# Two-layer hybrid recurrent trunk: gate weights stacked in one operand and interleaved with the first query tile, x loaded slice first, last tile and final norm by quarters

## The chip, the cores and the metric

The kernel runs on one core of a Trainium2 chip. The metric is device microseconds of one execution: the median of three runs before the change is 2355.97 us (2355.65 to 2356.04). A profile of one further execution stands beside them.

## The reference: what is computed

Two layers over 512 frames of width 1024, all in float32. Each layer normalises x (RMS), projects it with one large matrix, and feeds two branches, an mLSTM with four heads and a retention with four heads; a gated merge, a feed-forward block and a gated embedding are each added to x. At the end stands one more norm. What the change touches:

```python
h = rmsnorm(x, norm1_g[i])
z = h @ w_in[i] + b_in[i]
_, _, mv, mo, mi, mf, rq, rk, rv, rg, gm, gr = split_cols(z)   # mi, mf: 4 columns each
...
h3 = rmsnorm(x, norm3_g[i])
x = x + jax.nn.sigmoid(h3 @ w_pe_gate[i]) * (p[i] @ w_pe[i])   # the last step of a layer
return rmsnorm(x, final_g)
```

`mi` and `mf` are the input and forget gates of the mLSTM: 8 columns in all, of some 12,300.

## The kernel before

**Layout.** Activations lie transposed: eight tiles `x[0..7]` of 128 channels by 512 frames. Every float32 operand is split into a high part (`h`, a rounded copy, made by ScalarE, L286) and a low part (`l`, the rest, made by VectorE, L287), and every product is three matmuls: high by high, low by high, high by low (`mm3`, L423 to L425). An output tile of 128 channels (`t8`, L427) is 8 slices of 3 matmuls, 24 in all, each with 512 moving columns. The matmuls named in the profile by L423 to L425 are these.

**Weights.** They come in a fixed order of units (`unit_list`, L151): SyncE loads a block of 128x1024 (`wr`, 512 KB) into one of four or five raw buffers (`fill_raws`), ScalarE and VectorE split it into `wh` and `wl` two units ahead of its use (`unit`, `LOOK` = 2), in a ring of six buffers. All engines work in order, each on its own queue.

**Start.** TensorE runs 20 matmuls on ones (`WARM`, L863). SyncE loads the first weight block (unit `IF`: the 8 gate columns of the projection, set in a block of 128 columns that is zero otherwise), then x[0] to x[7]; ScalarE's queue loads the per-channel vectors `bc`. For each slice ScalarE makes `l0n1h` (L604) and VectorE `l0n1l` (L605): the operand is x times the gain, and the norm's factor is applied to the results later. TensorE then runs the gate tile (`l0if`, 24 matmuls, L911 to L913) and four query and key tiles of head 0 (`l0m0z`, L1155). Meanwhile ScalarE squares the slices (L618), and GpSimd adds up the squares (L626; the last one is added by VectorE, L624). After the second of those tiles TensorE sums over channels (`finish`, L633), VectorE and GpSimd form the factor, and after the third tile it is spread over the partitions (`spread`, L662). `gate_rows` (L783) then turns the gate tile into rows of decays with some twenty small operations on ScalarE and VectorE, and the evacuation of the query and key tiles follows on the same engines.

**Between the layers.** The last eight tiles of layer 0 (`l0pg`) are evacuated by `pe_evac` (L1417): multiply by the norm's factor, sigmoid, multiply by `pe`, add to x, then the operand of the next layer's norm (`l1n1h`, `l1n1l`). The gate tile and the query tiles of layer 1 follow at once.

**End.** In layer 1 the last four tiles are computed in two halves of 256 frames (`pl`, L1462), so that the final norm of the first half (`n40`) lies beside the matmuls of the second. For the second half (`n41`) stand at the very end: the evacuation of tile 7, its square, the sums over channels (L633, L635), the factor (VectorE, GpSimd, L640), two diagonal blocks (L648), a matmul that spreads them (L650), three multiplications (`final`, L1451) and their stores (L1452).

Of the kernel before, what the change touches and what calls it, by code (L numbers as in the profile page):

```python
# [42 lines left out]
P = 128  # L43
# [11 lines left out]
WARM = 20  # L55
# [180 lines left out]
def build(ctx, tc, ins, out):  # L236
# [34 lines left out]
    nc.scalar.dma_start(bc[:, 0, :], ins["vecs"][0])  # L271
# [85 lines left out]

    def fill_raws(most=RAWS + 1):
        while at["load"] < len(loads) and len(raws) + len(kept) < most:
# [20 lines left out]

    def prep_next():
# [10 lines left out]
        out_ = [pl.tile([P, w], F32R, name=f"w{a}{n}_{nm}", **kw) for a in "hl"]  # L392
# [3 lines left out]
        in_order("prep", *split(r[:, :w], *out_))  # L396
# [186 lines left out]
    class Norm:  # L583
# [23 lines left out]
        def square(self, k, x, pool=False):  # L607
# [7 lines left out]
            if pool:  # L615
                gp.tensor_tensor(sq, x, x, OP.mult)
            else:
                ac.activation(sq, x, AF.Square)  # L618
            if self.sum is None:
                self.sum = sq  # L620
            elif k == KT - 1 and self.n < NT:
                self.tail = sq
            elif k == KT - 1:
                ve.tensor_tensor(self.sum, self.sum, sq, OP.add)  # L624
            else:
                gp.tensor_tensor(self.sum, self.sum, sq, OP.add)  # L626

        def finish(self):
# [11 lines left out]
            gp.tensor_tensor(self.c[:, 0:self.n], ms, nhalf[:, 0:self.n], OP.pow)  # L640

# [141 lines left out]
    def gate_rows(i, o, nrm):  # L783
# [4 lines left out]
        ve.tensor_tensor(f[F_, :T], o[F_, :], nrm.b[F_, :], OP.mult)  # L788
        ac.activation(f[F_, :T], f[F_, :T], AF.Identity, bias=b[F_, :])
        li = tmp(n + "li")  # L790
        ve.tensor_tensor(li[I_, :T], o[I_, :], nrm.b[I_, :], OP.mult)
# [82 lines left out]
    for i in range(L):  # L874
# [279 lines left out]
        for d in range(4):  # L1154
            o = t8(xa, f"l{i}m0z{d}")  # L1155
# [293 lines left out]
    def final(n, c0, c1):  # L1449
        v = whole[:, c0:c1, n.s]  # L1450
        ve.tensor_tensor(v, v, n.b.rearrange("p (a t) -> p a t", a=1).to_broadcast([P, c1 - c0, n.n * P]), OP.mult)  # L1451
        nc.sync.dma_start(out[c0:c1, :, n.s].rearrange("c p t -> p c t"), v)  # L1452
# [6 lines left out]
    for a, n in enumerate(nn):  # L1459
        for c in range(KT - LAST, KT):  # L1460
# [8 lines left out]
            elif a == 1 and c == KT - LAST + 1:  # L1469
                nn[0].whole()  # L1470
            pe_evac(o, c, n.s, [n])
            ac.activation(x[c][:, n.s], x[c][:, n.s], AF.Copy, scale=n.col(c))
            if a == 1 and KT - LAST < c < KT - 1:
                final(nn[0], 4 * (c - KT + LAST - 1), 4 * (c - KT + LAST))
    nn[1].finish()
    nn[1].whole()
    for c0, c1 in ((0, 4), (4, 6), (6, 8)):
        final(nn[1], c0, c1)
# [8 lines left out]
def _pack_units(a):  # L1487
# [7 lines left out]
    for i in range(L):  # L1495
        for u in unit_list(i):
# [3 lines left out]
            elif u[0] in ("PAIR", "WIDE"):  # L1500
# [4 lines left out]
            elif u[0] == "PE":  # L1505
                c = 512 * u[1]
                blocks.append(a["w_pe"][i, :, c:c + T].reshape(2, P, 4, P).transpose(1, 2, 0, 3).reshape(P, UN))
            else:
                z = np.zeros((D, P), np.float32)
                z[:, 0:H] = a["w_in"][i, :, CI:CI + H]  # L1510
                z[:, 32:32 + H] = a["w_in"][i, :, CF:CF + H]
                put(z)
# [92 lines left out]
```

## Time and profile before

| what | us |
|---|---|
| median of three runs | 2355.97 |
| profiled execution, its own time | 2357.84 |
| span of that execution, first to last instruction | 2356.1 |
| TensorE busy in the span | 2328.2 |
| VectorE, ScalarE, GpSimd busy | 1716.9, 1217.9, 252.3 |
| first `l0if` matmul starts | 7.53 |
| `l0n1ss` (sum over channels) starts | 25.50 |
| first `l1if` matmul starts | 1181.57 |
| last matmul on weights starts | 2342.80 |
| last stores issued, DMA queue of SyncE ends | 2352.4 |

Rows of the timeline give the start in us from the span's start, the length in us, the engine, the line, the operation, output and inputs, and in brackets the idle time just before with what ended it. PE is TensorE, DVE VectorE, ACT ScalarE, POOL GpSimd, SP SyncE; a "q" behind a name is the engine's queue of DMA issues. Rows of the groups give busy us and mean ns. Windows give busy us and instructions of each engine in a stretch, then the granted TensorE clock, the DMA engines' share and GB/s. TensorE's matmuls overlap, so their pace is read from start to start.

### The profile page before, as it was taken

Reading aid. Unit: us, or ns where it says so; the run is one execution under the profiler, and the core shown is the slowest. Engines: PE = TensorE matmul, PEld = TensorE weight load, DVE = VectorE, ACT = ScalarE, POOL = GpSimd, SP = SyncE. Lnnn points to the kernel's source line nnn. Section 1 sums busy time; section 2 is a strip of 40 time slices with the busy share of each in tenths; the row PEclk is TensorE's granted clock in tenths of the full one; section 3 lists DMA queues with packets and bytes.
Section 4 is the critical chain, followed back from the end, with each engine's and each line's share of the span. In section 5 each row is a group of like instructions: output and inputs, shape, how many; then the busy total and the mean of one; then the engine's idle time right before and its main releaser. Section 6 shows DMA issues by size and latency. Waiting matters only on the chain. (4 is left out here: it accounts for less than half of the span.)

```text
span 2356.1 us, 35296 instructions
## 1 busy us (share of the span) xinstructions
PE 2328.2 (99%) x13692; PEld 2062.1 (88%) x13692; DVE 1716.9 (73%) x2643; ACT 1217.9 (52%) x1760; POOL 252.3 (11%) x372
## 2 busy tenths in 40 slices
PE   9999999999999999999999999999999999999998
PEld 7888899898898898898888888998989988998997
DVE  6877767886665586677768787778958656776785
ACT  5655544553454445445557564455536445445454
POOL 4111100100102200000321110000000020000012
PEclk9999999999999999999999999999999999999999
DMA  5666676666578766777776645334343443333431
GB/s 202 183 177 169 218 223 182 196 200 189 166 232 265 204 193 184 208 216 182 214 210 175 183 121 183 131 123 162 108 160 105 166 152 98 126 108 99 131 121 54
DMA packets 145319, 395.87 MB, mean 168 GB/s; under 512 B 14960, under 2 KB 17392, under 8 KB 145152
## 3 DMA queue, kind: packets, MB, share of 16 engines
q1 hardware_dynamic: 98928, 248.78, 32.1%
q0 software_dynamic: 31104, 117.45, 20.6%
q10 hardware_dynamic: 15120, 27.40, 3.3%
q8 instruction: 107, 1.75, 0.3%
q14 instruction: 60, 0.49, 0.1%
HBM read 374.69 MB, written 123.73 MB: 212 GB/s over the span
## 5 line engine op out<-in xcount | busy, mean ns | idle before, releaser
L286 ACT ACTIVATE wh<-wr 128x1024 fp32r<-128x1024 f32 x222 | 234.0, 1055 | 298.3 <-issue 64.9
L287 DVE TENSOR_TENSOR wl<-wr,wh 128x1024 fp32r<-128x1024 f32 x222 | 273.6, 1233 | 94.1 <-ACT wh L286 93.8
L286 ACT ACTIVATE wh_B<-wr 128x1024 fp32r<-128x1024 f32 x100 | 105.9, 1059 | 158.1 <-PE l0f L424 8.5
L287 DVE TENSOR_TENSOR wl_B<-wr,wh_B 128x1024 fp32r<-128x1024 f32 x100 | 122.1, 1221 | 31.0 <-ACT wh_B L286 30.8
L286 ACT ACTIVATE wh_D<-wr 128x512 fp32r<-128x512 f32 x76 | 48.0, 632 | 125.9 <-DVE wr L405 67.0
L286 ACT ACTIVATE wh_C<-wr 128x1024 fp32r<-128x1024 f32 x76 | 80.2, 1056 | 61.5 <-issue 8.4
L287 DVE TENSOR_TENSOR wl_C<-wr,wh_C 128x1024 fp32r<-128x1024 f32 x76 | 94.3, 1241 | 19.0 <-ACT wh_C L286 18.8
L286 ACT ACTIVATE wh_A<-wr 128x1024 fp32r<-128x1024 f32 x76 | 79.9, 1052 | 53.9 <-PE l1f L424 9.0
L287 DVE TENSOR_TENSOR wl_A<-wr,wh_A 128x1024 fp32r<-128x1024 f32 x76 | 92.8, 1221 | 17.2 <-ACT wh_A L286 16.7
L423 PE MATMUL l1f<-l1n2h,wh 128*128 128x512 f32 x256 | 99.8, 390 | 0.0
L423 PE MATMUL l0f<-l0n2h,wh 128*128 128x512 f32 x256 | 99.8, 390 | 0.0
L425 PE MATMUL l0f<-l0n2h,wl 128*128 128x512 f32 x256 | 99.7, 389 | 0.0
L425 PE MATMUL l1f<-l1n2h,wl 128*128 128x512 f32 x256 | 99.7, 389 | 0.0
L424 PE MATMUL l0f<-l0n2l,wh 128*128 128x512 f32 x256 | 99.6, 389 | 0.0
L424 PE MATMUL l1f<-l1n2l,wh 128*128 128x512 f32 x256 | 99.6, 389 | 0.0
L287 DVE TENSOR_TENSOR wl_D<-wr,wh_D 128x512 fp32r<-128x512 f32 x76 | 52.4, 690 | 33.7 <-ACT wh_D L286 32.1
L402 DVE TENSOR_TENSOR wr<-wr,wr 128x512 f32<-128x512 f32 x76 | 52.2, 687 | 16.0 <-DMA wr<-wpairs 14.4
L425 PEld LDWEIGHTS l0f<-l0n2h,wl 128*128 128x128 f32 x256 | 48.0, 188 | 10.2
L425 PEld LDWEIGHTS l1f<-l1n2h,wl 128*128 128x128 f32 x256 | 48.0, 188 | 10.2
L423 PEld LDWEIGHTS l0f<-l0n2h,wh 128*128 128x128 f32 x256 | 48.1, 188 | 9.8
L424 PEld LDWEIGHTS l1f<-l1n2l,wh 128*128 128x128 f32 x256 | 48.1, 188 | 9.8
L423 PEld LDWEIGHTS l1f<-l1n2h,wh 128*128 128x128 f32 x256 | 48.0, 188 | 9.7
(5613 smaller groups left out, 8370.1 us busy)
## 6 DMA issues: line engine op xcount, KB each, us to landing
wr<-wstream SPq DMA_DIRECT2D x222, 512.0 KB, 4.4
wr<-wpairs SPq DMA_DIRECT2D x228, 256.0 KB, 2.9
wr<-wwide SPq DMA_DIRECT2D x24, 512.0 KB, 3.6
s0t<-wwide POOLq DMA_DIRECT2D x5, 1024.0 KB, 7.9
s4t<-wwide POOLq DMA_DIRECT2D x5, 1024.0 KB, 8.9
s12t<-wwide POOLq DMA_DIRECT2D x5, 1024.0 KB, 8.6
s16t<-wwide POOLq DMA_DIRECT2D x5, 1024.0 KB, 8.7
s1t<-wpairs POOLq DMA_DIRECT2D x4, 1024.0 KB, 6.7
```

Source lines behind the costliest of these rows:

```text
L286: a = ac.activation(hi_ap, src, AF.Copy)
L287: return a, ve.tensor_sub(lo_ap, src, hi_ap.bitcast(F32))
L402: ve.tensor_tensor(raws[n, "B"][:, Q:], kept.pop((n, "A"))[:, Q:], r[:, :Q], OP.add)
L423: te.matmul(o, sh, mh, start=first, stop=False)
L424: te.matmul(o, sh, ml, start=False, stop=False)
L425: cur["mm"] = te.matmul(o, sl, mh, start=False, stop=last)
```

## The change

In both layers the gate weights are now a block of 128x64 (`wif`, 32 KB). One operand tile `z` is zeroed by GpSimd and holds, per slice, the high part in the columns from 0 and 32 and the low part in the columns from 64 and 96: so two matmuls per slice (one with the high activations, one with the low) give high and low products in different partitions of one PSUM tile. `gate_rows` adds the two parts with a ScalarE copy and a VectorE addition for each gate. The gate tile and the first query tile are now computed together, slice by slice. At the start x[0] is loaded before the first query weights, which come and are split in two halves; the vectors come in two pieces; the warm-up has 11 matmuls; the sums of squares of layer 0's first norm are added by VectorE. At the end tile 7's second half is evacuated in two quarters of 128 frames, and the final norm of the second half (`quarters`) is made for each quarter by itself, with stores of 8x128 and twice 4x128 columns in the place of 4x256 and twice 2x256.

The diff, with the packing on the host and plain renamings left out:

```diff
-WARM = 20
+WARM = 11
...
-    nc.scalar.dma_start(bc[:, 0, :], ins["vecs"][0])
+    nc.scalar.dma_start(bc[:, 0, 0:8], ins["vecs"][0][:, 0:8])
...
+    def halves(n):
+        return [slice(0, Q), slice(Q, UN)] if n == 1 else [slice(0, UN)]
...
+            elif units[n][0] == "IF":
+                eng = nc.sync if n else nc.scalar
+                eng.dma_start(r[:, 0:64], ins["wif"][n * L // NU])
             else:
-                in_order("load", nc.sync.dma_start(r, ins["wstream"][at["whole"]]))
+                w = ins["wstream"][at["whole"]]
+                for c in halves(n):
+                    in_order("load", nc.sync.dma_start(r[:, c], w[:, c]))
...
-        in_order("prep", *split(r[:, :w], *out_))
+        if gates:
+            z = out_[0]
+            gp.memset(z.bitcast(F32), 0.0)
+            z = z.rearrange("p (k g c) -> p k g c", g=4, c=32)
+            split(r[:, 0:64].rearrange("p (k g c) -> p k g c", g=2, c=H), z[:, :, 0:2, 0:H], z[:, :, 2:4, 0:H])
+        elif x == 0:
+            for c in halves(n):
+                in_order("prep", *split(r[:, c], *[a[:, c] for a in out_]))
...
-                gp.tensor_tensor(self.sum, self.sum, sq, OP.add)
+                (add or gp).tensor_tensor(self.sum, self.sum, sq, OP.add)
...
+        def quarters(self):
+            n = self.name
+            o = [ps(f"{n}ss{j}") for j in range(self.n)]
+            r = []
+            for part in (self.sum, self.tail):
+                for j in range(self.n):
+                    te.matmul(o[j][:, 0:2], part[:, j * P:(j + 1) * P], ones[:, 0:2], start=part is self.sum,
+                              stop=part is self.tail)
+            for j in range(self.n):
+                ms = cols.tile([P, NT], F32, name=f"{n}ms{j}", tag="ms")[:, 0:1]
+                ve.tensor_scalar(ms, o[j][:, 0:1], 1.0 / D, EPS, OP.mult, OP.add)
+                c = cols.tile([P, NT], F32, name=f"{n}rc{j}", tag="rc")[:, 0:1]
+                gp.tensor_tensor(c, ms, nhalf[:, 0:1], OP.pow)
+                r.append(c)
+            for j, c in enumerate(r):
+                d = tmp(f"{n}d{j}")[:, 0:P]
+                ve.tensor_scalar(d, ident, c, None, OP.mult)
+                r[j] = ps(f"{n}rp{j}")[:, 0:P]
+                te.matmul(r[j], ones, d, start=True, stop=True)
+            return r
...
-        ve.tensor_tensor(f[F_, :T], o[F_, :], nrm.b[F_, :], OP.mult)
+        li = tmp(n + "li")
+        for d_, s_, e_ in ((f, F_, slice(96, 96 + H)), (li, I_, slice(64, 64 + H))):
+            ac.activation(d_[s_, :T], o[e_, :], AF.Copy)
+            ve.tensor_tensor(d_[s_, :T], o[s_, :], d_[s_, :T], OP.add)
+        ve.tensor_tensor(f[F_, :T], f[F_, :T], nrm.b[F_, :], OP.mult)
...
-    fill_raws(1)
-    for k in range(KT):
+    nc.sync.dma_start(x[0], ins["xT"][0])
+    fill_raws(2)
+    nc.scalar.dma_start(bc[:, 0, 8:NB], ins["vecs"][0][:, 8:NB])
+    for k in range(1, KT):
         nc.sync.dma_start(x[k], ins["xT"][k])
     ready(0)
-    for k in range(KT):
+    n1.operand(0, x[0])
+    ready(1)
+    for k in range(1, KT):
         n1.operand(k, x[k])
...
-        _, wh, wl = unit("IF")
+        _, wi = unit("IF")
+        _, wh, wl = unit("T8")
         og = ps(f"l{i}if")
+        oz = ps(f"l{i}m0z0")
         for k in range(KT):
             s = slice(k * P, (k + 1) * P)
-            mm3(og, wh[:, s], wl[:, s], xa[0][k], xa[1][k], k == 0, k == KT - 1)
+            f, e = k == 0, k == KT - 1
+            te.matmul(og, wi[:, s], xa[0][k], start=f, stop=False)
+            te.matmul(og, wi[:, s], xa[1][k], start=False, stop=e)
+            mm3(oz, wh[:, s], wl[:, s], xa[0][k], xa[1][k], f, e)
         if i == 0:
             for k in range(KT):
-                n1.square(k, x[k])
+                n1.square(k, x[k], ve)
...
-            o = t8(xa, f"l{i}m0z{d}")
+            o = t8(xa, f"l{i}m0z{d}") if d else oz
...
+    def last_evac(o, n):
+        c = KT - 1
+        js = [(slice(j * P, (j + 1) * P), slice((j - 2) * P, (j - 1) * P)) for j in (2, 3)]
+        t = [tmp(f"plt{j}")[:, 0:P] for j in range(2)]
+        n.tail = tmp("pltail")[:, 0:2 * P]
+        for a, (s, q) in zip(t, js):
+            ve.tensor_tensor(a, o[:, q], n3.b[:, s], OP.mult)
+            ac.activation(a, a, AF.Sigmoid)
+        for a, (s, q) in zip(t, js):
+            ve.tensor_tensor(a, a, pe[:, c, s], OP.mult)
+        for a, (s, q) in zip(t, js):
+            ve.tensor_tensor(x[c][:, s], x[c][:, s], a, OP.add)
+            ac.activation(n.tail[:, q], x[c][:, s], AF.Square)
+        for s, q in js:
+            ac.activation(x[c][:, s], x[c][:, s], AF.Copy, scale=n.col(c))
...
+            if a == 1 and c == KT - 1:
+                last_evac(o, n)
+                break
...
-    nn[1].finish()
-    nn[1].whole()
-    for c0, c1 in ((0, 4), (4, 6), (6, 8)):
-        final(nn[1], c0, c1)
+    for j, (b, ends) in enumerate(zip(nn[1].quarters(), ((0, KT), (0, KT // 2, KT)))):
+        for c0, c1 in zip(ends, ends[1:]):
+            final(slice((2 + j) * P, (3 + j) * P), b, c0, c1)
```

How the instructions stand now, at the three places of which the prediction speaks. TensorE at the start, before: the gate tile `l0if` by itself, three matmuls per slice.

```order
L864 MATMUL warm<-ones_r 128x128 x20
L423 MATMUL l0if<-l0n1h_157,wh_0_212 128x512
L424 MATMUL l0if<-l0n1l_158,wh_0_212 128x512
L425 MATMUL l0if<-l0n1h_157,wl_0_213 128x512
L423 MATMUL l0if<-l0n1h_159,wh_0_212 128x512
```

And after (`wh_0_205` is the stacked gate operand, `l0m0z` the first query tile; the numbers behind `l0n1h` and `l0n1l` tell the slices apart):

```order
L905 MATMUL warm<-ones_r 128x128 x11
L961 MATMUL l0if<-l0n1h_157,wh_0_205 128x512
L962 MATMUL l0if<-l0n1l_158,wh_0_205 128x512
L442 MATMUL l0m0z_271<-l0n1h_157,wh_0_213 128x512
L443 MATMUL l0m0z_271<-l0n1l_158,wh_0_213 128x512
L444 MATMUL l0m0z_271<-l0n1h_157,wl_0_214 128x512
L961 MATMUL l0if<-l0n1h_159,wh_0_205 128x512
```

Five matmuls now use a slice where three did, and the first query tile ends with the gate tile. Layer 1 has the same order at its start.

VectorE at the start, before, from the operand of the last slice (`l0n1l_172`) to the first operation on the norm's sum over channels (`l0n1ms`):

```order
L605 SCALAR_TENSOR_TENSOR l0n1l_172<-x_150,bc,l0n1h_171 128x512
L287 TENSOR_TENSOR wl_0_260<-wr_204,wh_0_259 128x1024
L287 TENSOR_TENSOR wl_0_266<-wr_206,wh_0_265 128x1024
L624 TENSOR_TENSOR l0n1sum<-l0n1sum,l0n1sq_314 128x512
L287 TENSOR_TENSOR wl_0_345<-wr_208,wh_0_344 128x1024
L888 CAST l0sel<-l0selraw 36x512
L287 TENSOR_TENSOR wl_0_376<-wr_210,wh_0_375 128x1024
L637 TENSOR_SCALAR l0n1ms<-l0n1ss 128x4
```

And after, the same stretch:

```order
L624 SCALAR_TENSOR_TENSOR l0n1l_172<-x_150,bc,l0n1h_171 128x512
L642 TENSOR_TENSOR l0n1sum<-l0n1sum,l0n1sq_314 128x512
L642 TENSOR_TENSOR l0n1sum<-l0n1sum,l0n1sq_317 128x512
L287 TENSOR_TENSOR wl_0_261<-wr_199,wh_0_260 128x1024
L642 TENSOR_TENSOR l0n1sum<-l0n1sum,l0n1sq_320 128x512
L287 TENSOR_TENSOR wl_0_267<-wr_201,wh_0_266 128x1024
L642 TENSOR_TENSOR l0n1sum<-l0n1sum,l0n1sq_323 128x512
L642 TENSOR_TENSOR l0n1sum<-l0n1sum,l0n1sq_326 128x512
L642 TENSOR_TENSOR l0n1sum<-l0n1sum,l0n1sq_329 128x512
L287 TENSOR_TENSOR wl_0_363<-wr_203,wh_0_362 128x1024
L933 CAST l0sel<-l0selraw 36x512
L640 TENSOR_TENSOR l0n1sum<-l0n1sum,l0n1sq_332 128x512
```

Six additions of squares that GpSimd made now stand among the weight splits, and the last addition stands behind three splits where it stood behind two.

VectorE at the end, before, from the evacuation of tile 7 (`pl`) on:

```order
L1420 TENSOR_TENSOR l1pgt_256_23107<-pl_23082,l1n3rb 128x256
L1422 TENSOR_TENSOR l1pgt_256_23107<-l1pgt_256_23107,l1pe 128x256
L1423 TENSOR_TENSOR l1x<-l1x,l1pgt_256_23107 128x256
L637 TENSOR_SCALAR l1n41ms<-l1n41ss 128x2
L648 TENSOR_SCALAR l1n41d<-ident,l1n41rc 128x128 x2
L1451 TENSOR_TENSOR l1x<-l1x,l1n41rp 128x4x256
L1451 TENSOR_TENSOR l1x<-l1x,l1n41rp 128x2x256 x2
```

And after:

```order
L1511 TENSOR_TENSOR plt_23094<-pl_23069,l1n3rb 128x128
L1511 TENSOR_TENSOR plt_23095<-pl_23069,l1n3rb 128x128
L1514 TENSOR_TENSOR plt_23094<-plt_23094,l1pe 128x128
L1514 TENSOR_TENSOR plt_23095<-plt_23095,l1pe 128x128
L1516 TENSOR_TENSOR l1x<-l1x,plt_23094 128x128
L1516 TENSOR_TENSOR l1x<-l1x,plt_23095 128x128
L669 TENSOR_SCALAR l1n41ms_23115<-l1n41ss_23109 128x1
L669 TENSOR_SCALAR l1n41ms_23119<-l1n41ss_23110 128x1
L675 TENSOR_SCALAR l1n41d_23123<-ident,l1n41rc_23117 128x128
L675 TENSOR_SCALAR l1n41d_23127<-ident,l1n41rc_23121 128x128
L1501 TENSOR_TENSOR l1x<-l1x,l1n41rp_23125 128x8x128
L1501 TENSOR_TENSOR l1x<-l1x,l1n41rp_23129 128x4x128 x2
```

Each step on 256 frames has become two on 128, and the first final multiplication needs only the first quarter's factor. Elsewhere the engines' orders differ only by the operations that the diff names.

More of the change, by code (lines that the diff above doesn't have):

```diff
@@ L391, in prep_next @@
         nm = f"{x[0]}{x[1]}" if wide else x
-        out_ = [pl.tile([P, w], F32R, name=f"w{a}{n}_{nm}", **kw) for a in "hl"]
+        gates = units[n][0] == "IF"
+        out_ = [pl.tile([P, w], F32R, name=f"w{a}{n}_{nm}", **kw) for a in ("h" if gates else "hl")]
         r = formed.pop((n, x), None)
@@ L395, in prep_next @@
             r = raws.pop((n, x))
-        in_order("prep", *split(r[:, :w], *out_))
+        if gates:
[6 more added lines that the diff above has]
+                in_order("prep", *split(r[:, c], *[a[:, c] for a in out_]))
+        else:
+            in_order("prep", *split(r[:, :w], *out_))
         pieces[n, x] = out_
@@ L1504, in _pack_units @@
                 put(a["w_in"][i, 256 * k:256 * k + 256, c:c + T])
-            elif u[0] == "PE":
+            else:
                 c = 512 * u[1]
                 blocks.append(a["w_pe"][i, :, c:c + T].reshape(2, P, 4, P).transpose(1, 2, 0, 3).reshape(P, UN))
[L1508 to L1512, printed above, removed]
     return np.stack(blocks)
```

24 lines of the change are left out of this document (11 added, 13 removed).

## The prediction

> **What bounds the kernel now.** I read the page's sum first, then the windows by stage, then TensorE's waits.
>
> ```profile
> span 2356.1 us, 35296 instructions
> PE 2328.2 (99%) x13692; PEld 2062.1 (88%) x13692; DVE 1716.9 (73%) x2643; ACT 1217.9 (52%) x1760; POOL 252.3 (11%) x372
> 0.00:26.00 26.00, 24.18 (x118) 20.39 (x118) 13.56 (x15) 16.22 (x23) 19.84 (x42) 1.00 0.72 260
> 60.00:1160.00 1100.00, 1088.86 (x6453) 966.83 (x6452) 805.16 (x1233) 563.86 (x815) 128.18 (x176) 1.00 0.69 200
> 1215.00:2336.00 1121.00, 1117.82 (x6670) 994.68 (x6669) 831.52 (x1285) 587.27 (x855) 80.34 (x116) 1.00 0.43 133
> 2343.10:2356.10 13.00, 2.44 (x10) 1.54 (x10) 4.33 (x9) 1.82 (x5) 1.43 (x2) 0.64 0.24 81
> ```
>
> TensorE has work in 99% of the span; in the long middle (60 to 1160, 1215 to 2336) it idles 14 of 2221 us. So an edit counts only where it takes matmuls from TensorE, or where TensorE idles or runs for nothing: the first 26 us (warm-up until 7.5, waits for the first operands) and the last 13 us, where it works 2.44. The change touches these two places and takes 8 matmuls in each layer. A shift of everything behind is worth its full length, since the middle follows TensorE.
>
> **The start, before.** The rows are the first weight block, the slices, the pace of TensorE and the sum over channels.
>
> ```profile
> 1.05 6.73 PE L864 MATMUL warm<-ones_r 128*128 128x128 f32 x40 [1.05 <-POOL ones_r L275]
> 4.89 1.06 ACT L286 ACTIVATE wh<-wr 128x1024 fp32r<-128x1024 f32 x1 [2.37 <-DMA wr<-wstream]
> 7.35 4.05 ACT L604 ACTIVATE l0n1h<-x,bc 128x512 fp32r<-128x512 f32 x6 [0.17 <-DMA x<-xT]
> 7.53 0.47 PE L423 MATMUL l0if<-l0n1h,wh 128*128 128x512 f32 x1
> 13.44 0.50 PE L423 MATMUL l0m0z<-l0n1h,wh 128*128 128x512 f32 x1
> 17.34 0.39 PE L423 MATMUL l0m0z<-l0n1h,wh 128*128 128x512 f32 x1
> 18.02 0.39 PE L423 MATMUL l0m0z<-l0n1h,wh 128*128 128x512 f32 x1
> 22.40 0.69 DVE L624 TENSOR_TENSOR l0n1sum<-l0n1sum,l0n1sq 128x512 f32<-128x512 f32 x1 [5.28 <-POOL l0n1sum L626]
> 25.50 0.95 PE L633 MATMUL l0n1ss<-ones_r,l0n1sum 128*128 128x2 f32 x8
> ```
>
> Matmuls of 512 columns start every (18.02 − 17.34)/3 = 0.227 us. The gate tile starts at 7.53; the first query tile at 13.44, with a hole at its beginning; the sum over channels, `l0n1ss`, at 25.50, right behind the second query tile, and its operand has been ready since 23.1. What counts is therefore when `l0n1ss` starts after the change, as everything behind it keeps its order.
>
> **The start, after.** Two queues can set that point.
>
> ```profile
> 6.00:8.00 2.00, 2.00 (x18) 1.77 (x17) 2.00 (x3) 1.83 (x4) 2.00 (x4) 1.00 1.05 398
> L605 DVE SCALAR_TENSOR_TENSOR l0n1l<-x,bc,l0n1h 128x512 fp32r<-128x512 f32 x8 | 5.4, 738 | 0.0
> L287 DVE TENSOR_TENSOR wl<-wr,wh 128x1024 fp32r<-128x1024 f32 x222 | 273.6, 1233 | 94.1 <-ACT wh L286 93.8
> 24.17 0.43 DVE L888 CAST l0sel<-l0selraw 36x512 fp32r<-36x512 f32 x1
> ```
>
> *TensorE's.* The first weights, 512 KB, were usable at 4.89. x[0] has half of that: usable between 2.5 (half the time) and 4.9 (none of it saved, if the start of the transfers is all that counts); I take 4.2, in the upper half, since no row shows a start-up time apart. ScalarE's high part (0.72, as at 1187.33 below) and VectorE's low part (0.74) follow, then the small gate block (estimate 0.25, as of the 1.06 for 1024 columns at L286 little more than 0.2 can fall on 64): TensorE starts at about 5.9, and the 11 warm-ups end near it (11/20 of 6.7 us gives 4.8; all at their slow first pace 5.8). ScalarE waited for x[2] at 7.35; ahead of x[2] then were 512 KB of weights and two slices, as now, so x[2] is usable at 7.35 again. With 0.72 and 0.74 behind it, TensorE is through with slice 2 at about 9.7. The other five slices arrive faster (262 thousand bytes at 398 GB/s, 0.66 us) than TensorE uses them (5 matmuls, 1.13 us): both tiles end at 9.7 + 5.7 = 15.4, the next query tile 24 × 0.227 = 5.45 later, at **20.85**.
>
> *VectorE's.* x[7] is usable at 7.35 + 5 × 0.66 = 10.65; high and low parts make it 12.1. Behind that stand seven additions of squares (0.69), three weight splits (1.23) and a cast (0.43), one starting some 0.07 before its forerunner's end: 4.8 + 3.7 + 0.45 less 0.7, about 8.3. The sum is ready at **20.5**, with ScalarE's squares no later. The two ends nearly tie; `l0n1ss` starts at about 21.1, a gain of **4.4 us**. Bounds: 5.2 if nothing waits; 0.9 for the half-rate start below.
>
> The hole at the query tile's beginning before was a wait for its split weights; these now come in halves, ahead of the slices but the first. The additions on ScalarE and VectorE in `gate_rows` (two copies, two sums of 512 columns) stand in front of splits that wait anyway:
>
> ```profile
> 32.96 1.23 DVE L287 TENSOR_TENSOR wl<-wr,wh 128x1024 fp32r<-128x1024 f32 x1 [2.09 <-ACT wh L286]
> PE l0m0vp L709 <- DVE wl L287: 1.2, 1, 1.2
> ```
>
> VectorE idles 2.09 us there, and the two sums take, at the 0.69 of L624's row with as many columns, 1.4; ScalarE idles longer still, as that split waits for it and it for TensorE. So I cost them at nothing. Without that cover they would delay VectorE's queue by 1.4 and TensorE's one later wait of this stage (1.2 us, for a split) by as much. The first norm's squares leave GpSimd, which has nothing else that is late. In layer 1 GpSimd zeroes a 128x1024 tile ahead of two additions; it is 11% busy, and nothing waits there.
>
> **Between the layers.**
>
> ```profile
> 1181.57 0.39 PE L423 MATMUL l1if<-l1n1h,wh 128*128 128x512 f32 x1
> 1187.33 0.72 ACT L604 ACTIVATE l1n1h<-l0x,bc 128x512 fp32r<-128x512 f32 x1 [1.49 <-DVE l0x L1423]
> 1188.08 0.75 DVE L605 SCALAR_TENSOR_TENSOR l1n1l<-l0x,bc,l1n1h 128x512 fp32r<-128x512 f32 x1 [0.79 <-ACT l1n1h L604]
> 1188.11 0.50 PE L423 MATMUL l1if<-l1n1h,wh 128*128 128x512 f32 x1
> 1192.89 0.39 PE L423 MATMUL l1m0z<-l1n1h,wh 128*128 128x512 f32 x1
> ```
>
> From 1181.57 TensorE runs the 48 matmuls of gate tile and first query tile; the next tile starts at 1192.89. That is 11.32 us for 48 × 0.227 = 10.9: 0.4 goes where the last slice, ready at 1188.05 and 1188.83, comes late. After the change 40 matmuls need 9.1 us, and the last slice is used only after 35 of them, at 1189.5 on this clock, so it is in time. Gain 11.3 − 9.1 = **2.2 us** (1.8, the 8 matmuls alone, if a wait returns).
>
> **The end.**
>
> ```profile
> 2342.80 0.28 PE L425 MATMUL pl<-l1n3h,wl 128*128 128x256 f32 x1
> 2343.11 0.42 DVE L1420 TENSOR_TENSOR l1pgt<-pl,l1n3rb 128x256 f32<-128x256 f32 x1 [0.44 <-PE pl L425]
> 2345.51 0.38 PE L635 MATMUL l1n41ss<-ones_r,l1n41sq 128*128 128x2 f32 x2 [1.02 <-ACT l1n41sq L618]
> 2346.62 0.71 POOL L640 TENSOR_TENSOR l1n41rc<-l1n41ms,nhalf 128x2 f32<-128x2 f32 x1 [2.57 <-DVE l1n41ms L637]
> 2347.36 0.48 DVE L648 TENSOR_SCALAR l1n41d<-ident,l1n41rc 128x128 f32<-128x128 f32 x2 [0.82 <-POOL l1n41rc L640]
> 2347.89 1.22 PE L650 MATMUL l1n41rp<-l1n41d,ones_r 128*128 128x256 f32 x2 [1.55 <-DVE l1n41d L648]
> 2349.15 2.42 DVE L1451 TENSOR_TENSOR l1x<-l1x,l1n41rp 128x1024 f32<-128x1024 f32 x3 [1.31 <-PE l1n41rp L650]
> 2351.00:2353.00 2.00, 0.00 (x0) 0.00 (x0) 0.57 (x1) 0.00 (x0) 0.00 (x0) 0.50 0.86 284
> 14.60:14.75 0.15, 0.00 (x0) 0.00 (x0) 0.15 (x1) 0.15 (x1) 0.15 (x1) 1.00 0.77 263
> ```
>
> From 2343.11 the chain takes 2.40 to the square's sum, 6.04 to the first final multiplication, 8.46 to the last one's end. With 128 frames a step on VectorE or ScalarE takes about 0.28 (the pair at 2347.36 needs 0.48 for two, against 0.42 for one of 256). The first quarter passes five steps, with the second's step between some of them, in 1.95 in place of 2.40. Its two sums no longer stand behind the other quarter's (0.4 saved); GpSimd's power takes 0.7 as before; one diagonal block is 0.28 in place of 0.48 (0.2); the spreading matmul has half the columns (estimate 0.7, a little over half of 1.22). First final multiplication: 6.04 − 0.45 − 0.4 − 0.2 − 0.5 = 4.5, **1.55 earlier**; the second quarter's chain ends inside its 1.2 us. Multiplications and stores behind it have the same volume. But the stores then run without a hole for three microseconds (284 GB/s in a window that they do not fill), so their rate sets the end, and their rows shrink from 1024 to 512 bytes. Same bytes per time would cost 0, same rows per time 3.1. The only place with rows of 512 bytes is the load of `ident` at 14.6, 263 GB/s with the DMA engines at a share of 0.77, which at a full share is no slower than the stores are: I take 0.25, near zero. Gain **1.3 us** (−1.5 to 2.0).
>
> **Sum.** 4.4 + 2.2 + 1.3 = 7.9 us. The profiled execution's own time, 2357.84 for a span of 2356.1, would become 2349.9; the median of the runs is 1.9 lower than that execution, and I put the gain on it: 2355.97 − 7.9 = **2348.1**.
>
> **The clock.** The granted clock is where another result may come from.
>
> ```profile
> 1.90:5.30 3.40, 3.40 (x18) 1.00 0.91 313
> 5.30:7.50 2.20, 2.20 (x21) 1.00 1.02 383
> 605.00:609.40 4.40, 0.05 (x1) 1.00 0.96 377
> 609.40:616.40 7.00, 6.61 (x30) 0.51 0.12 43
> PE l0r2o1a L472 <- ACT wh_A L286: 4.4, 1, 4.4
> ```
>
> Until 5.3 TensorE passes 18 warm-up records in 3.4 us, then 21 in 2.2: twice the pace, though the column shows 1.00. And behind the one long wait (4.4 us, to 609.4) the clock is half for 7.0 us, although TensorE was busy 6.61 of them. The Trainium skill, "TensorE: Matmul & The Clock Gate", Part 1, says that the clock is half until a free-running window of about 3.4 us was busy throughout, and that the window doesn't begin with the kernel. Both rows agree; the rule speaks against 11 warm-ups, since they last hardly a window and a half.
>
> **Rivals.**
> - *Half rate at the start.* The warm-ups end near 5.5 and TensorE then idles between slices 0, 1 and 2. If a clock that is half needs the 7 us of the row above, from about 6.9 on, TensorE is slow until 13.9: 8.0 us at 0.454 are 17 matmuls, the other 23 take 5.2, both tiles end at 19.1 in place of 15.4, `l0n1ss` comes at 24.6. Start 0.9, all 4.4: 2351.6. For it: half rate held through 94% busy; against it: in this execution the clock rose at 5.3, before the warm-ups end. 0.15.
> - *VectorE becomes the bound of the start.* The adds come behind splits that wait for TensorE's buffers; if the sum is ready at 23 and not at 20.5, the start gives 2.4 and all is 5.9: 2350.1. For it: VectorE has no hole between 12 and 20.5 in my sum; against it: what it waits for is early. 0.13.
> - *The half clock at 609 disappears.* The wait before it stays, but all is moved by 4.4 us, and if the clock then doesn't fall, the 6.61 us of work run at full rate: 3.3 more, 2344.8. For it: the clock fell only at the very end of that wait, at 609.4, so a little less would not do; against it: if executions differ in this at random, the medians don't. 0.12.
> - *Slower.* The clock stays half far beyond the start, because each small hole denies it: it costs 0.5 us for each us, so the gain of 7.9 is gone after some 16 us of half rate beyond 5.9, and slower by 0.2% needs 25, to the third query tile at 31. For it: the 7 us above; against it: TensorE runs without a hole from slice 3 on. 0.04.
>
> **How the numbers follow.** Forecast, gain 6.3 to 9.3: 0.56. The range takes in the forecast, the early clock and the late VectorE down to a gain of 4.8: 2344.8 to 2351.2, over 0.8 in all. A measurement here can tell about 0.2%, 4.7 us, from no change. Faster by more: 0.56 + 0.12 + 0.13 and a little of the first rival, 0.83; within: 0.13; slower: 0.04.
>
> **What would show it.** `l0n1ss` at 21 (24.6 with a granted clock of 0.5 near 8 to 13: first rival; a wait of `l0n1ss` for VectorE: second); 40 matmuls in 9.1 us at the layer boundary without a wait; the last weight matmul 6.6 us earlier in the span; the first final multiplication 4.5 us behind it and the last store's rate near 300 GB/s. Wrong would be: x[0] later than 4.9, a wait in `l0m0vp` beyond 1.2, or another hole of 4 us.

## The result, and the profile after

The changed kernel takes 2348.75 us (median of nine runs, 2347.34 to 2351.17), the kernel before beside it 2355.45 (nine runs, 2353.66 to 2356.97): a ratio of 0.9971, with a 95% interval of 0.9962 to 0.998. That is 6.7 us less, where 7.9 were predicted and 2348.1 stood as the time.

The profiled execution of the changed kernel took 2347.49 with a span of 2345.8, 10.3 less than the span of before. That is more than the medians differ: it lies at the lower end of the change's nine runs, and the one of before, 2357.84, above all nine of its own. So the terms are read from stretches, not from the spans. First the start, TensorE's rows and those of the engines that feed it (start in us, length, engine, line; in brackets the idle time before and what ended it):

```profile
1.05 4.63 PE L905 MATMUL warm<-ones_r 128*128 128x128 f32 x22 [1.05 <-POOL ones_r L275]
3.63 1.28 ACT L623 ACT_TABLE_LOAD   x1 [3.63 <-DMA x<-xT]
4.93 0.72 ACT L623 ACTIVATE l0n1h<-x,bc 128x512 fp32r<-128x512 f32 x1
6.35 0.22 DVE L287 TENSOR_TENSOR wh<-wr,wh 128x64 fp32r<-128x64 f32 x1
6.62 0.50 PE L961 MATMUL l0if<-l0n1h,wh 128*128 128x512 f32 x1 [0.94 <-DVE wh L287]
16.10 0.39 PE L442 MATMUL l0m0z<-l0n1h,wh 128*128 128x512 f32 x1
20.66 0.67 DVE L640 TENSOR_TENSOR l0n1sum<-l0n1sum,l0n1sq 128x512 f32<-128x512 f32 x1
21.54 0.95 PE L649 MATMUL l0n1ss<-ones_r,l0n1sum 128*128 128x2 f32 x8
```

x[0] is there at 3.63, earlier than predicted, but ScalarE then loads its function table for 1.28 us. With the old start (the row is from `e2_tail_only` below) that load lay in the wait for the first weights; now it stands behind the wait for x[0]:

```profile
1.24 1.28 ACT L286 ACT_TABLE_LOAD   x1 [1.24 <-PEq L1637]
```

The first gate matmul comes at 6.62, both tiles end at 16.10, and `l0n1ss` starts at 21.54 in place of 25.50. The sum's last addition ends at 21.33: VectorE and TensorE tie, as predicted.

Between the layers (the first gate matmul, the last slice on ScalarE and on TensorE, the next tile's first matmul, and the sum over channels):

```profile
1175.03 0.39 PE L961 MATMUL l1if<-l1n1h,wh 128*128 128x512 f32 x1
1181.64 0.72 ACT L623 ACTIVATE l1n1h<-l0x,bc 128x512 fp32r<-128x512 f32 x1 [1.49 <-DVE l0x L1473]
1182.96 0.39 PE L961 MATMUL l1if<-l1n1h,wh 128*128 128x512 f32 x1
1184.25 0.40 PE L442 MATMUL l1m0z<-l1n1h,wh 128*128 128x512 f32 x1
1189.73 0.95 PE L649 MATMUL l1n1ss<-ones_r,l1n1sum 128*128 128x2 f32 x8
```

Forty matmuls take 9.22 us where 48 took 11.32: 2.1 saved, and no bracket says that TensorE waited. To `l1n1ss` it is 14.70.

The end (VectorE's evacuation of tile 7 in quarters, the power, the spreading matmuls, the final multiplications, and a window from the last multiplication on):

```profile
2333.83 0.49 DVE L1511 TENSOR_TENSOR plt<-pl,l1n3rb 128x128 f32<-128x128 f32 x2 [0.45 <-PE pl L444]
2336.48 1.09 POOL L671 TENSOR_TENSOR l1n41rc<-l1n41ms,nhalf 128x1 f32<-128x1 f32 x2 [1.71 <-DVE l1n41ms L669]
2337.41 1.39 PE L677 MATMUL l1n41rp<-l1n41d,ones_r 128*128 128x128 f32 x4 [0.99 <-DVE l1n41d L675]
2338.31 2.42 DVE L1501 TENSOR_TENSOR l1x<-l1x,l1n41rp 128x1024 f32<-128x1024 f32 x3 [0.43 <-PE l1n41rp L677]
2340.80:2342.80 2.00, 0.00 (x0) 0.00 (x0) 0.00 (x0) 0.00 (x0) 0.00 (x0) 0.50 1.02 285
```

The first final multiplication starts 4.48 behind the evacuation (6.04 before; 4.5 predicted). But the last one's end lies 5.1 before the span's end (4.5 in the kernel before), and from the evacuation to the span's end it is 11.97 in place of 12.99: of the 1.56 only 1.0 is left. In the window, which they fill, the stores with rows of 512 bytes move 285 GB/s.

In the middle the long wait stands where it stood, and the clock is halved there as before:

```profile
PE l0r2o1a L491 <- ACT wh_A L286: 3.4, 1, 3.4
602.70:609.40 6.70, 5.26 (x23) 4.97 (x24) 5.04 (x11) 3.89 (x9) 0.00 (x0) 0.51 0.45 158
```

### The profile page after: what moved, and what is told of

It reads as the page before. It is cut to its first block, busy times and chain, and to the rows that moved or that the text cites. A ratio compares the mean times of both kernels' runs of the same rounds, so it can differ in the third digit from the quotient of the medians.

```text
span 2345.8 us, 35261 instructions
## 1 busy us (share of the span) xinstructions
PE 2320.2 (99%) x13660; PEld 2056.2 (88%) x13660; DVE 1722.9 (73%) x2658; ACT 1218.9 (52%) x1768; POOL 245.7 (10%) x369
## 5 line engine op out<-in xcount | busy, mean ns | idle before, releaser
L286 ACT ACTIVATE wh<-wr 128x1024 fp32r<-128x1024 f32 (+1 forms) x223 | 232.2, 1044 | 276.5 <-issue 69.6
L287 DVE TENSOR_TENSOR wl<-wr,wh 128x1024 fp32r<-128x1024 f32 (+1 forms) x221 | 271.9, 1232 | 77.7 <-ACT wh L286 77.5
```

What stands on the lines that cost most here:

```text
L286: a = ac.activation(hi_ap, src, AF.Copy)
L287: return a, ve.tensor_sub(lo_ap, src, hi_ap.bitcast(F32))
```

## The experiments

All runs of one group lie on the same chip beside runs of the kernel before, whose median is 2358.03 in the first group (28 runs), 2355.77 in the second (18) and 2356.96 in the third (23). Differences below are against these. The change itself ran beside the others in the second group alone (`e0_again`).

### The end alone, undone and done (first group)

`e1_old_tail`, the change without its end:

```diff
-            if a == 1 and c == KT - 1:
-                last_evac(o, n)
-                break
...
-    for j, (b, ends) in enumerate(zip(nn[1].quarters(), ((0, KT), (0, KT // 2, KT)))):
-        for c0, c1 in zip(ends, ends[1:]):
-            final(slice((2 + j) * P, (3 + j) * P), b, c0, c1)
+    nn[1].finish()
+    nn[1].whole()
+    for c0, c1 in ((0, 4), (4, 6), (6, 8)):
+        final(nn[1].s, nn[1].b, c0, c1)
```

> The changed kernel with the old end (tile 7's second half and its norm on 256 frames at once). Theory, three separate terms on TensorE's path (start 4.0, layer boundary 2.1, end 1.05 by the two traces): only the end is undone, so 1.05 us slower than the change, 5.7 us faster than before; first final multiplication 6.0 us behind the first evacuation of tile 7, span ends 13.0 behind it. Rival, the stores set the end and the quarters bring nothing: as fast as the change, 6.7 us faster than before, with the span's end 12.0 behind the evacuation here too.

`e2_tail_only` is the opposite: the kernel before with these lines as the change has them.

> The kernel before with the new end alone. Theory: 1.05 us faster than before (2354.4), first final multiplication 4.5 us behind the first evacuation of tile 7, span's end 12.0 behind it. Rival, the quarters only move the wait to the stores: no change, span's end 13.0 behind the evacuation.

Measured: 2350.41 for the first (ratio 0.9968, 0.9956 to 0.9979), 2356.44 for the second (0.9994, 0.9985 to 1.0003). One microsecond is below what these intervals tell apart; the traces tell it. First the evacuation and the final multiplications of `e1_old_tail` and its span, then those of `e2_tail_only`:

```profile
2334.49 0.42 DVE L1470 TENSOR_TENSOR l1pgt<-pl,l1n3rb 128x256 f32<-128x256 f32 x1 [0.44 <-PE pl L444]
2340.53 2.42 DVE L1501 TENSOR_TENSOR l1x<-l1x,l1n41rp 128x1024 f32<-128x1024 f32 x3 [1.31 <-PE l1n41rp L688]
span 2347.4 us, 35248 instructions
```

```profile
2341.17 0.49 DVE L1483 TENSOR_TENSOR plt<-pl,l1n3rb 128x128 f32<-128x128 f32 x2 [0.44 <-PE pl L425]
2345.36 2.42 DVE L1473 TENSOR_TENSOR l1x<-l1x,l1n41rp 128x1024 f32<-128x1024 f32 x3
span 2352.9 us, 35309 instructions
```

With the old end the multiplications start 6.04 behind the evacuation and the span ends at 12.9; with the new one 4.19 and 11.7. So the end is worth 1.0 us in the changed kernel (12.9 against 11.97) and about 1.25 in the kernel before (12.99 against 11.7), and the rival, that the stores take it back, holds for a third of it only.

### The eight gate matmuls (first group)

`e3_third_gate` adds a matmul per slice whose result nobody reads:

```diff
             te.matmul(og, wi[:, s], xa[1][k], start=False, stop=e)
+            te.matmul(oy, wi[:, s], xa[0][k], start=f, stop=e)
```

> The changed kernel with one more gate matmul per slice in both layers (into a tile that nobody reads), 16 in all. Theory, matmuls on TensorE's path set the start and the boundary: 16 x 0.227 = 3.6 us slower than the change, 3.1 faster than before; l0n1ss at 23.3 in place of 21.54, and 16.5 us from the first l1if to l1n1ss in place of 14.7. Rival, VectorE's sum of squares (ready at 21.3) sets the start: the eight of layer 0 are covered, l0n1ss stays near 21.5 to 22, the kernel is only 1.8 to 2.2 slower than the change.

Measured: 2351.89 (0.998, 0.9971 to 0.9989).

```profile
23.27 0.95 PE L649 MATMUL l0n1ss<-ones_r,l0n1sum 128*128 128x2 f32 x8
1176.90 0.39 PE L962 MATMUL l1if<-l1n1h,wh 128*128 128x512 f32 x1
1193.22 0.95 PE L649 MATMUL l1n1ss<-ones_r,l1n1sum 128*128 128x2 f32 x8
```

The boundary takes 16.32, 1.62 longer than in the change: nearly the whole 8 × 0.227 = 1.8. `l0n1ss` comes at 23.27, which is 1.73 later than in the first trace of the change, but only 1.0 later than the average of the four traces with this start (22.3, see the next experiment). VectorE's sum was ready at 21.76 and TensorE didn't wait for it, so matmuls lie on the path there too, and the rival (covered by VectorE's sum) is out for this execution; how much of the 1.8 the start pays, one trace can't tell. The whole time shows a smaller loss than the 3.6 expected: the kernel is 6.1 faster than before by the medians and 4.7 by the ratio, where the theory said 3.1.

### The order of the loads (first group)

`e4_old_loads` puts x[0] behind the whole first weight block again:

```diff
-WARM = 11
+WARM = 20
...
-        return [slice(0, Q), slice(Q, UN)] if n == 1 else [slice(0, UN)]
+        return [slice(0, Q), slice(Q, UN)] if n < 0 else [slice(0, UN)]
...
-    nc.sync.dma_start(x[0], ins["xT"][0])
     fill_raws(2)
+    nc.sync.dma_start(x[0], ins["xT"][0])
```

> The changed kernel with the old start of the loads: x[0] behind the whole first weight block, no halves, 20 warm-ups. Theory, the start's gain comes from five matmuls per arriving slice in place of three, the load order only sets the first of them: first gate matmul near 7.6 (6.62 in the change), both tiles end near 16.8, l0n1ss near 22.3, 0.8 to 1 us slower than the change. Rival, the order of the loads carries the start: holes between the slices return, l0n1ss at 24 or later, 2.5 us or more slower than the change.

Measured: 2351.39 (0.9971, 0.9962 to 0.998). The rows are the table load, now behind the wait for the small gate weights, the first gate matmul and the sum:

```profile
5.56 1.28 ACT L286 ACT_TABLE_LOAD   x1 [5.56 <-DMA wr<-wif]
8.30 0.48 PE L961 MATMUL l0if<-l0n1h,wh 128*128 128x512 f32 x1
23.70 0.95 PE L649 MATMUL l0n1ss<-ones_r,l0n1sum 128*128 128x2 f32 x8
```

`l0n1ss` at 23.70 lies between the two theories. Four traces with the change's own start have it at 21.54, 22.37, 22.72 and 22.48, on average 22.3, and two with the old start at 25.5 and 25.6. So by this one trace the old start of the loads costs about 1.4 of the start's 3.3, and the other 1.9 remain with what the edit leaves in place: the stacking with the interleaving, and the additions on VectorE. The edit undoes the order, the halves and the number of warm-ups together, and the table load behind a landing took part in the loss too; the experiment doesn't separate these. The whole time doesn't show the 1.4 at all: the ratio is the change's own, 0.9971, and its interval is wider than that.

### The change again, and fewer warm-ups (second group)

> The changed kernel once more, beside the next three on the same chip: 6.7 us faster than before, l0n1ss between 21.5 and 22.4 (the two starts seen so far differ by 0.8, as the slices of x land at other times).

Measured: 2349.92, 5.9 us less than before (0.9971, 0.996 to 0.9983). This trace shows what differs from execution to execution at the start: the second half of the first weights, and x[7], land later than in the first trace, and TensorE now waits for the sum of squares. The last row, a window at the start, is for comparison with the next run.

```profile
6.88 0.63 ACT L286 ACTIVATE wh<-wr 128x512 fp32r<-128x512 f32 x1 [0.44 <-DMA wr<-wstream]
12.54 0.72 ACT L623 ACTIVATE l0n1h<-x,bc 128x512 fp32r<-128x512 f32 x1 [0.38 <-DMA x<-xT]
22.72 1.05 PE L649 MATMUL l0n1ss<-ones_r,l0n1sum 128*128 128x2 f32 x8 [0.34 <-DVE l0n1sum L640]
6.70:10.10 3.40, 3.08 (x11) 1.95 (x12) 3.01 (x5) 3.12 (x5) 2.97 (x7) 1.00 1.01 380
```

`e5_warm3` has 3 warm-ups:

```diff
-WARM = 11
+WARM = 3
```

> The changed kernel with 3 warm-ups in place of 11. Theory, the clock is granted by windows of about 3.4 us that run free of the kernel, after one that was busy (in five traces it rose between 4.4 and 7.1 us): the warm-ups end near 2.3, so the first busy window lies in the gate tile; TensorE runs at half pace from 6.6 for 3.4 to 6.8 us, l0n1ss comes at 23.2 to 25, the kernel is 1.7 to 3.4 us slower than the change. Rival, some matmuls at the start are enough whatever their number: l0n1ss at 21.5 to 22.4, no difference.

Measured: 2351.76 (0.998, 0.9971 to 0.9989), 1.8 more than the change beside it. The warm-ups, the first gate matmul, the sum, and two windows (the matmuls of TensorE stand in the first pair of brackets):

```profile
1.05 1.65 PE L905 MATMUL warm<-ones_r 128*128 128x128 f32 x6 [1.05 <-POOL ones_r L275]
6.72 0.79 PE L961 MATMUL l0if<-l0n1h,wh 128*128 128x512 f32 x1 [4.02 <-DVE wh L287]
22.89 0.95 PE L649 MATMUL l0n1ss<-ones_r,l0n1sum 128*128 128x2 f32 x8
6.70:10.10 3.40, 3.38 (x8) 2.71 (x9) 3.40 (x6) 3.40 (x7) 3.38 (x6) 1.00 1.06 399
10.20:12.20 2.00, 2.00 (x10) 1.65 (x9) 1.87 (x4) 2.00 (x4) 2.00 (x5) 1.00 0.99 396
```

Eight matmuls in 3.4 us, then ten in 2.0: half pace until about 10. `l0n1ss` is at 22.89 although the slices came early here (VectorE's sum was ready at 21.35). So the first rival of the prediction is real and has this price; with eleven warm-ups or more it was not seen in twelve traces. By the traces' clock records the clock rose between 4.2 and 6.9 us in those twelve, and at 10.0 in this one, 3.3 behind the first gate matmul. The Trainium skill, "TensorE: Matmul & The Clock Gate", Part 1, says that the clock doubles after one busy window of some 3.4 us that runs free of the kernel. This agrees with all thirteen, but the window needn't be busy throughout, as the prediction took it: in `e1_old_tail` the clock rose at 6.74, and TensorE had been busy for 2.78 of the 3.41 us before.

### The table load (second and third group)

`e6_table_early` puts a tiny activation in front, so that the table is loaded while x[0] is on its way:

```diff
     nc.scalar.dma_start(bc[:, 0, 8:NB], ins["vecs"][0][:, 8:NB])
+    early = cols.tile([P, NT], F32, name="early", tag="early")
+    ac.activation(early, nhalf, AF.Copy)
...
-    ready(0)
     n1.operand(0, x[0])
     ready(1)
```

> The changed kernel with one activation of 4 columns in front of ScalarE's first real one, so that the table load (1.28 us, behind the wait for x[0] in the change) lies in that wait. Theory, the table load is on the path to the first matmul: first gate matmul at 5.3 to 5.7 in place of 6.6, l0n1ss up to 1.0 earlier (20.6), the kernel 0.7 to 1.0 us faster than the change. Rival, the landing of the next slices or VectorE's sum sets l0n1ss: first gate matmul as early, but l0n1ss still at 21.3 or later, no gain.

Measured: 2363.39 (1.0031, 1.0019 to 1.0043), 13.5 us more than the change: neither theory had this. The start is as the rival said: first gate matmul at 5.70, then a wait, as the second half of the weights lands at 6.6, and `l0n1ss` at 22.76. The loss lies behind it, in stretches that the edit doesn't touch: 758.7 us from `l1n1ss` to `l1n2ss`, against 754.2 in the change beside it, and TensorE idles only 0.5 more there. In that stretch the 512-column matmuls of the tiles `l1bm`, for example, start every 0.233 us in place of 0.227. The new tile is 16 bytes per partition, but by the layout of the two kernels it moved all tiles laid out behind it by 64: the first weights of `l1bm` lie at byte 42528 in place of 42464, and its activations, which are laid out from the other side, at 122848 in both.

`e10_table_in_place` is made to tell that apart:

```diff
-    early = cols.tile([P, NT], F32, name="early", tag="early")
+    early = cols.tile([P, NT], F32, name="early", tag="ms")
```

> The kernel of e6_table_early with its 16-byte result in a buffer that exists already, in place of a tile of its own: all instructions stand in the same order on all engines, only the tiles laid out behind that tile lie 64 bytes lower, as in the change. Theory, the place of the operands in SBUF cost e6 its 13 us (matmuls of 512 columns every 0.233 us in place of 0.227 wherever weights and activations had moved against each other by 64 bytes): pace 0.227 again, as fast as the change to 1 us, l0n1ss near 22.8 as in e6 (the second half of the first query weights lands at 6.6). Rival, the changed order on ScalarE and VectorE at the start is carried on: still 2363.

Measured: 2350.61 (0.9971, 0.996 to 0.9981). One piece of TensorE's work at the same place of layer 0's feed-forward block, first in `e6_table_early`, then in `e10_table_in_place`, and last a piece of layer 1's block in `e6_table_early`; from the first to the second row of each pair are five steps from matmul to matmul:

```profile
999.61 0.39 PE L444 MATMUL l0f<-l0n2h,wl 128*128 128x512 f32 x1
1000.78 0.39 PE L443 MATMUL l0f<-l0n2l,wh 128*128 128x512 f32 x1
```

```profile
999.67 0.39 PE L444 MATMUL l0f<-l0n2h,wl 128*128 128x512 f32 x1
1000.80 0.39 PE L443 MATMUL l0f<-l0n2l,wh 128*128 128x512 f32 x1
```

```profile
2160.56 0.39 PE L444 MATMUL l1f<-l1n2h,wl 128*128 128x512 f32 x1
2161.70 0.39 PE L443 MATMUL l1f<-l1n2l,wh 128*128 128x512 f32 x1
```

Five steps take 1.17 in the first pair, 1.13 in the second. All instructions of the two kernels stand in the same order on every engine, so the place of the tiles is shown as the cause. The third pair, 1.14, is a control inside one execution: in layer 1 both operands of this block have moved by 64, and the pace is the usual one. With the layout of the change and of `e6_table_early` set beside the starts of their matmuls, some 9,300 gaps behind matmuls of 512 columns whose two operands agree modulo 128 bytes are 0.2274 us on average, and some 3,060 where they differ by 64 are 0.2329. `e6_table_early` has about 2,580 of the second kind and the change 480, so this explains some 12 of the 13 us. The change's own 480 cost it some 2.7 us; the kernel before has them too.

What the table load was worth is shown by three more rows of `e10_table_in_place`:

```profile
5.57 0.50 PE L962 MATMUL l0if<-l0n1h,wh 128*128 128x512 f32 x1
6.60 0.63 ACT L286 ACTIVATE wh<-wr 128x512 fp32r<-128x512 f32 x1 [0.91 <-DMA wr<-wstream]
7.14 0.61 ACT L634 ACTIVATE l0n1sum<-x 128x512 f32<-128x512 f32 x1
```

The first gate matmul comes 1.1 earlier than in the change, but ScalarE then waits for the second half of the weights until 6.60, and `l0n1ss` is at 22.28, the average of the four. (In three of those four ScalarE waits for that half too, until 6.80 to 6.99, with the table load in its old place.) The edit also changed the order: ScalarE now squares x[0] at 7.14, before it makes x[1]'s operand, for which TensorE waits until 8.41. So the load was on the path to the first matmul, and the landing of the weights, with that square behind it, takes its 1.1 back; the two are not separated.

### Who adds the squares (third group)

`e7_gpsimd_sum`:

```diff
-                n1.square(k, x[k], ve)
+                n1.square(k, x[k])
```

> The changed kernel with the sum of squares of layer 0's first norm back on GpSimd (VectorE only the last addition). Theory, the move to VectorE is worth something only as the sum would else come last: six additions of 1.29 to 1.66 us from 12.4 on end at 22.2, the last one at 22.9, l0n1ss at 22.9 to 23.3 waiting for it, 0.4 to 1.4 us later than in the change. Rival, VectorE's queue was itself the bound: without the additions l0n1ss comes at 21.5 or earlier.

Measured: 2351.89 (0.9978, 0.9969 to 0.9987). VectorE's last addition, and the sum over channels:

```profile
23.07 0.69 DVE L640 TENSOR_TENSOR l0n1sum<-l0n1sum,l0n1sq 128x512 f32<-128x512 f32 x1 [5.27 <-POOL l0n1sum L642]
23.82 1.05 PE L649 MATMUL l0n1ss<-ones_r,l0n1sum 128*128 128x2 f32 x8 [1.91 <-DVE l0n1sum L640]
```

TensorE waits 1.91 us for the sum, which is ready at 23.77, later than the 22.9 expected. Compared with the average of 22.3, without the move of the additions to VectorE the faster gate tile would have given back 1.5 of the 3.3 us of the start.

### Rows of 1024 bytes, and a version from all this (second and third group)

`e9_long_rows` keeps the quarters and changes the last multiplications and stores:

```diff
+    q0, q1 = nn[1].quarters()
+    for c0, c1 in ((0, 4), (4, 8)):
+        for j, b in enumerate((q0, q1)):
+            v = whole[:, c0:c1, (2 + j) * P:(3 + j) * P]
+            ve.tensor_tensor(v, v, b.rearrange("p (a t) -> p a t", a=1).to_broadcast([P, c1 - c0, P]), OP.mult)
+        nc.sync.dma_start(out[c0:c1, :, 2 * P:4 * P].rearrange("c p t -> p c t"), whole[:, c0:c1, 2 * P:4 * P])
```

> The changed kernel with the same quarters, but the final multiplications as four of 4x128 columns and two stores of 4x256 (rows of 1024 bytes) in place of three stores with rows of 512. Theory, the short rows cost the end 0.5 us (5.1 us from the last multiplication to the span's end, 4.5 before): 4.5 to 4.6 again, span's end 11.4 behind the first evacuation of tile 7 in place of 12.0, 0.5 us faster than the change. Rival, only the bytes count: the last store is now larger and starts later, so the same or up to 0.5 us slower.

Measured: 2349.32 (0.9972, 0.996 to 0.9983).

```profile
2336.15 0.49 DVE L1511 TENSOR_TENSOR plt<-pl,l1n3rb 128x128 f32<-128x128 f32 x2 [0.44 <-PE pl L444]
2340.26 2.48 DVE L1549 TENSOR_TENSOR l1x<-l1x,l1n41rp 128x512 f32<-128x512 f32 x4
2342.80:2344.80 2.00, 0.00 (x0) 0.00 (x0) 0.00 (x0) 0.00 (x0) 0.00 (x0) 0.50 1.03 342
span 2347.3 us, 35259 instructions
```

The stores move 342 GB/s in place of 285, the last multiplication ends 4.6 before the span's end in place of 5.1, and the end is 11.1 long in place of 11.97. So rows of 512 bytes cost 0.5. It isn't the number of the stores: the kernel before and `e1_old_tail`, with three stores of rows of 1024 bytes, move 343 and 344 GB/s in such a window. (0.3 more of the difference are the spreading matmuls, 1.08 us here and in `e2_tail_only`, 1.39 in the change, whose clock is already halved at that point.) Its end is 0.8 shorter than the change's; the medians, 0.6 apart, can't tell the two kernels apart.

`e11_all` joins the table load in place, the long rows, four pieces of the first weights each behind a slice, and the first three additions on GpSimd:

```diff
-                for c in halves(n):
+                for j, c in enumerate(halves(n)):
                     in_order("load", nc.sync.dma_start(r[:, c], w[:, c]))
+                    if n == 1 and j < 3:
+                        in_order("load", nc.sync.dma_start(cur["x"][1 + j], ins["xT"][1 + j]))
...
-                n1.square(k, x[k], ve)
+                n1.square(k, x[k], gp if k < 4 else ve)
```

> A version from the runs so far: table load in place as in e10, the first query weights in four pieces, each loaded behind the slice that uses it, the first three additions of squares on GpSimd, the last four on VectorE, and the end with rows of 1024 bytes. Theory, each of the small terms counts: first gate matmul at 5.4 to 5.9, no hole between the slices, l0n1ss at 20.5 to 21.3, end 11.1 us behind the first evacuation of tile 7: 1.5 to 2.5 us faster than the change. Rival, the DMA stream sets the start: the slices land as late as before, l0n1ss at 22 or later, and only the 0.8 of the end remains.

Measured: 2352.45 (0.998, 0.9971 to 0.9988), some 2 more than the change by the ratios. GpSimd's two additions, VectorE's first one, and TensorE's wait:

```profile
15.20 2.65 POOL L644 TENSOR_TENSOR l0n1sum<-l0n1sum,l0n1sq 128x512 f32<-128x512 f32 x2
17.88 0.69 DVE L644 TENSOR_TENSOR l0n1sum<-l0n1sum,l0n1sq 128x512 f32<-128x512 f32 x1 [3.62 <-ACT l0n1sq L636]
19.76 0.50 PE L446 MATMUL l0m0z<-l0n1h,wl 128*128 128x512 f32 x1 [2.60 <-DVE wl L287]
```

Both theories failed: the start lost elsewhere. GpSimd's additions stood behind small operations of its own queue and ended at 17.85; the fourth addition, VectorE's first, waited for them (the bracket names ScalarE's square, which had long been done), and the weight split that stands behind it on VectorE's queue was late for TensorE by 2.60. `l0n1ss` came at 26.5. The finer loads were not told apart by this run; both tiles ended where they end in the change.

## Why the prediction was right, and where its sizes were off

The range, the sign and the three places were right; each term was somewhat too large.

- *Start, 4.4 predicted, 3.3 measured* (25.55 on average less 22.3; 3.96 in the first pair of traces). What the sum had wrong is TensorE's first matmul "at about 5.9", measured at 6.62 to 6.93. The table load (1.28 us) is missing in it: it lost its cover, as the wait that it stood beside became a wait that it stands behind. That the first matmul is late by less than that, 0.7 to 1.0, is luck: x[0] was there at 3.63 to 3.94 and not at 4.2. In three of the four traces the landings are late besides: ScalarE waits for the second half of the first weights until 6.80 to 6.99, and in one of them for x[7] until 12.54, against 10.65 predicted. Why they land later was not tried. (Four weight blocks are issued behind the slices, but they were so in the kernel before too; in those three executions SyncE issued the slices themselves more slowly, and these blocks from 7.37 to 7.55 on, in place of 6.82.)
- *VectorE's chain, ready at 20.5 predicted*: 21.33 and 22.66 in the two traces of the change. Its length behind the last slice was nearly right, 8.6 in both for 8.3; its beginning, 12.1 predicted, was late: 12.73 and 14.05. In the second trace x[7] landed late; in the first ScalarE didn't wait for it, but came to it only at 11.2, behind the table load and a square of x[0] on its own queue. The second rival, VectorE as the bound, is true in two of four traces (brackets of 0.34 and 0.16 us; 0.5 and 0.3 by the pace of the matmuls), not by 2.
- *`gate_rows` for nothing*: the wait behind it, of `l0m0vp`, is 1.3 and 1.4 in place of 1.2. That is 0.1 to 0.2 beyond the sign that the prediction set for itself, so nearly nothing.
- *Boundary, 2.2*: 2.1, without a wait, and the price of the matmuls there confirmed from the other side by `e3_third_gate`.
- *End, 1.3*: 1.0 to 1.25. The first final multiplication was right to 0.02 in the first trace, where the clock was already halved at the spreading matmuls; where it falls later (`e2_tail_only`) it comes 0.3 earlier. The term that was mis-sized is the short rows, put at 0.25 and measured at 0.5: it was read from a window of 0.15 us in which `ident` was loaded, and the rate there didn't hold for stores.
- *Clock*: the half rate behind the long wait did not disappear (third rival); a stretch of half clock stands in that place in every trace. The first rival's stretch at the start has not been seen with 11 warm-ups.

3.3, 2.1 and 1.1 make 6.5, and the medians differ by 6.7. The rest of the 10.3 between the two profiled executions (3.96, 2.06 and 1.02 make 7.0) lies in the middle, which the change doesn't touch. One wait there, of `l0r2o1a`, is 4.4 and 3.4, and it was anywhere from 3.4 to 4.4 in the traces of this study. What sets that wait from execution to execution wasn't tried.

## What to carry to other kernels

When an edit takes a wait away, look at what was hidden in that wait, a function table's load among it, and put that somewhere early on its own; then ask which transfer is next. Count a chain that moves to another engine with everything that stands behind it on that in-order queue. And before an edit that adds even a small tile is judged, compare the pace of the untouched stages: a moved layout can cost more than the edit is worth.

## What the runs showed of the hardware that was not expected

- Matmuls of 512 columns whose two operands lie 64 bytes apart modulo 128 in a partition start every 0.233 us, those whose operands agree every 0.227. A 16-byte tile that shifted one side by 64 made the kernel 13 us slower (2363.39 against 2350.61 with the same instructions in the same order).
- Stores with rows of 512 bytes ran at 282 to 285 GB/s in nine traces, with rows of 1024 at 342 to 344 in four (two microseconds from the last multiplication on). The Trainium skill, "DMA: Bandwidth & Descriptors", Specifications, gives 512 bytes as enough for the full rate; these stores don't agree.
- A single hole of 2.60 us, up to 19.76, halved the clock again from 20.3 to 23.8 in `e11_all`, by the trace's clock record; in `e6_table_early` one of 1.84 us, up to 2301.28, was followed by half clock from 2302.8 to 2306.2.
